# Attention of a streaming encoder layer: units of four key blocks, maxima between the scores, VectorE in written order

## The chip, the core and the metric

The kernel runs on one core of a Trainium2 chip. A core has TensorE (PE, matrix products into PSUM), VectorE (DVE), ScalarE (ACT) and GpSimd (POOL) for elementwise work, and SyncE (SP), whose queue issues the transfers between memory and SBUF. The metric is the device time of one execution in microseconds.

## The reference

One inference step of a layer with two branches, for a prompt of 2048 tokens and 64 decoded tokens that follow a cache of 512. One input projection (3080 columns) feeds an S5 branch (width 512) and an attention branch (8 heads of 64 with a forget bias); both are gated, concatenated, and go through one output projection. The part that the change touches:

```python
def _fox_attend(q, cum_q, pos_q, k, v, cum_k, pos_k):
    s = jnp.einsum('bqhd,bkhd->bhqk', q, k).astype(jnp.float32) * ATTN_SCALE
    s = s + jnp.transpose(cum_q, (0, 2, 1))[:, :, :, None] - jnp.transpose(cum_k, (0, 2, 1))[:, :, None, :]
    mask = pos_k[None, :] <= pos_q[:, None]
    s = jnp.where(mask[None, None], s, -jnp.inf)
    p = jax.nn.softmax(s, axis=-1)
    return jnp.einsum('bhqk,bkhd->bqhd', p.astype(v.dtype), v)
```

The prompt attends to itself, causally; the decoded tokens attend to the cache and to themselves. All is float32.

## The kernel before

The stages follow each other: input projection and the S5 scan (to about 724 us in the trace), the S5 branch's sigmoid gate, "GLU" (724 to 790), attention (790 to 1217), and the output product (to the end).

**Work of attention.** The heads are taken in four pairs `hp`, the two heads of a pair on two halves of the partitions or of PSUM. For each pair come five query tiles `qt`: 4 stands for the decoded tokens, 0 to 3 for 512 queries each of the prompt. Keys come in blocks of 128, four to a "kind" (the cache, a quarter of the prompt, or the new tokens). A tile's work per key block:

- *scores* (`scores`): four matmul pairs into a "twin", a PSUM tile [128, 2, 512] from a ring of three. Keys stand on the partitions. The pair `sm`, `kb` adds the biases and subtracts each query's maximum; `qs`, `ks` are the high and low parts of queries and keys (three products). A causal block gets mask products more. ScalarE takes the exponential of the twin into `p`. Scores are row-tiled (64x128: two matmuls on two halves of the rows).
- *values* (`mix`): the products of `p` with `vt`, column-tiled (128x64), gathered over the tile's blocks in one PSUM bank `po`. Two blocks form a unit (`PVG`), and the values of a unit come after the scores of the *next* one (`pend`).
- *additions*: the denominators need the sum of all `p`; VectorE and GpSimd add them in turn (`i % 2`, partial blocks on VectorE) into two `acc`, which are joined, and `sums` multiplies with ones, at a later unit. The result is scaled into `z` and stored for the output product.

**Maxima** (`maxima`): ahead of a tile's scores its maxima must be known. For 128 queries and a kind of keys, one matmul pair (high parts only) writes a twin, and VectorE adds the bias `cb` (loaded by SP and spread over the partitions) and takes the maximum, once for each head (line 1411, output `pb` into a scratch tile, `pm` the maximum). Two such steps go with each unit of two blocks (one after each block's scores), and two with each of the sixteen steps of GLU (`MXU`). When the last is done, `mq` is written, transposed on TensorE and copied to `sm`.

**Transposes** (`turn`): loaded keys and queries (`kn`) are transposed on TensorE into the PSUM bank `tr`; ScalarE copies the high part, VectorE subtracts for the low part (line 1375). One turn follows each unit, unless `sums` stands there.

**Order.** TensorE runs in the order in which the code is written (`Chain` with `strict`); on the other engines a scheduler orders the ready instructions. Buffers that are held for a time (`hold`, `claim`, `can`) are keyed by the tile's place in the order.

**Output weights.** Once nothing is left to load, the generator `Out.weights` is advanced by two steps after each unit: a weight tile is loaded into `ost` (a ring of three), split by a cast on ScalarE (`ohb`) and a subtraction on GpSimd (`olb`), two loads later. The output product itself begins after attention.

## Time and profile before

| | us |
|---|---|
| median of 3 runs (lowest, highest) | 1391.43 (1388.07, 1394.94) |
| profiled execution | 1393.23 |
| its span | 1391.4 |
| TensorE, VectorE, ScalarE, GpSimd busy | 1312.5, 968.5, 652.0, 520.5 |
| attention, 790 to 1217: TensorE, VectorE, ScalarE, GpSimd busy | 405.1, 317.0, 205.5, 163.9 |

The mean granted clock of TensorE is 0.981. Busy time on TensorE counts a matmul from its start to its modelled end, slow clock included. Line 154 is the chain's `matmul`, so groups of TensorE are told apart by their tiles: `twin<-sm,kb` begins a block of scores, `twin<-qs,ks` are its other products, `twin<-ks,qs` with 128 queries as weights is a maximum, `bank<-p,vt` are values, `bank<-ident,kn` and `bank<-identr,mq` transposes, `bank<-acc,ones` sums.

### The profile page before, as it was taken

What the parts mean: (1) busy time and instruction counts of PE and PEld (TensorE: products, weight loads), DVE (VectorE), ACT (ScalarE), POOL (GpSimd) and SP (SyncE); (2) the same over time, 40 slices, a digit from 0 to 9 for tenths busy, and PEclk for the clock granted to TensorE, in tenths of its full rate; (3) what the DMA queues carried; (4) which work ended last, traced back from release to release, by engine and by line L of the source; (5) the groups of instructions that cost most, each with busy time, mean ns of one, the idle gap of its engine ahead of it and who ended that gap; (6) DMA issues with size and microseconds to landing.
All of it is one profiled execution on the core that took longest, in us unless ns stands there. A gap on an engine that the chain in (4) does not pass through costs nothing.

```text
span 1391.4 us, 25886 instructions
## 1 busy us (share of the span) xinstructions
PE 1312.5 (94%) x9164; PEld 1031.9 (74%) x9164; DVE 968.5 (70%) x2404; ACT 652.0 (47%) x1710; POOL 520.5 (37%) x502
## 2 busy tenths in 40 slices
PE   5888999999999899999999899999999989898998
PEld 2886999998889899998879755555555554387887
DVE  3635896977877679864218877786787885446775
ACT  3645356567453576573315335445445445522211
POOL 1100254556534354452004113423423426743453
PEclk9899999999999999999999889999999999999999
DMA  9885333543546836446249624134121133495552
GB/s 342 318 309 124 100 86 94 154 123 107 163 133 217 282 110 180 145 141 196 84 138 291 202 73 121 32 91 125 43 70 48 40 65 79 146 330 169 182 164 78
DMA packets 249476, 204.92 MB, mean 147 GB/s; under 512 B 91296, under 2 KB 217340, under 8 KB 248322
## 3 DMA queue, kind: packets, MB, share of 16 engines
q1 hardware_dynamic: 249346, 203.27, 47.6%
q8 instruction: 72, 1.18, 0.4%
q14 instruction: 58, 0.48, 0.1%
HBM read 137.68 MB, written 65.53 MB: 146 GB/s over the span
## 4 chain that ended last, share of the span: by engine, by line
PE 63%; DVE 11%; DMA 6%; POOL 4%; issue 4%; ACT 3%; SPq 1%; DVEq 0%; ACTq 0%; POOLq 0%
PE low L154 25%; PE twin L154 13%; PE bank L154 12%; PE last L154 7%; PE glu L154 3%; DVE pb L1411 2%; PE bank L157 2%; DMA wst<-in_w_in_dram 1%; POOL qss L329 1%; POOL olb L205 1%; DMA lt<-t 1%; DVE acc L1489 1%; ACT p L354 1%; DVE ev L650 1%; DVE wlo L323 1%
## 5 line engine op out<-in xcount | busy, mean ns | idle before, releaser
L154 PE MATMUL low<-whi,h 128*128 128x256 f32 (+1 forms) x1584 | 296.3, 285 | 6.5 <-DVE th L609 3.5
L154 PE MATMUL low<-h,whi 128*128 128x256 f32 (+2 forms) x1152 | 277.6, 332 | 0.4 <-DVE h L323 0.3
L154 PEld LDWEIGHTS low<-whi,h 128*128 128x128 f32 x1584 | 247.9, 189 | 10.0 <-DVE th L609 3.7
L1411 DVE CUSTOM_DVE_ANT_0 pb<-twin,cb 128x512 bf16<-128x512 f32 (+3 forms) x328 | 199.9, 609 | 58.9 <-PE twin L154 49.1
L154 PE MATMUL low<-wlo,h 128*128 128x256 f32 (+1 forms) x816 | 229.1, 283 | 5.9 <-DVE wlo L323 5.9
L154 PEld LDWEIGHTS low<-h,whi 128*128 128x128 f32 x1152 | 195.5, 192 | 21.4 <-issue 2.8
L354 ACT ACTIVATE p<-twin 128x1024 f32<-128x1024 f32 (+3 forms) x180 | 149.7, 839 | 119.4 <-PE twin L154 107.2
L154 PE MATMUL low<-h,wlo 128*128 128x256 f32 (+2 forms) x576 | 188.2, 327 | 1.2 <-DVE wlo L323 1.2
L154 PEld LDWEIGHTS low<-wlo,h 128*128 128x128 f32 x816 | 154.3, 189 | 8.2 <-DVE wlo L323 7.7
L154 PE MATMUL bank<-p,vt 128*64 128x512 f32 (+3 forms) x704 | 142.5, 527 | 0.0
L154 PE MATMUL twin<-qs,ks 64*128 64x512 f32 (+3 forms) x1056 | 134.1, 359 | 0.0
L154 PEld LDWEIGHTS low<-h,wlo 128*128 128x128 f32 x576 | 110.3, 192 | 10.9 <-DVE wlo L323 2.6
L323 DVE TENSOR_TENSOR wlo<-wst,whi 128x512 fp32r<-128x512 f32 (+1 forms) x96 | 71.6, 752 | 59.9 <-ACT whi L319 59.7
L1489 DVE TENSOR_TENSOR acc<-acc,p 128x1024 f32<-128x1024 f32 (+4 forms) x88 | 90.2, 1025 | 30.5 <-ACT p L354 28.1
L329 POOL TENSOR_TENSOR qss<-qss,mhalf 128x4 f32<-128x4 f32 (+1 forms) x68 | 79.9, 1176 | 84.1 <-DVE qss L328 76.0
L154 PEld LDWEIGHTS twin<-qs,ks 64*128 64x128 f32 x1056 | 95.2, 191 | 11.0
L154 PE MATMUL twin<-sm,kb 64*128 64x512 f32 (+3 forms) x360 | 78.0, 428 | 21.2 <-DVE pm L1411 14.4
L319 ACT CAST whi<-wst 128x512 fp32r<-128x512 f32 (+1 forms) x96 | 58.7, 619 | 73.2 <-PE low L154 37.5
L154 PEld LDWEIGHTS bank<-p,vt 128*64 128x64 f32 x704 | 45.2, 140 | 63.8 <-issue 56.1
L205 POOL TENSOR_TENSOR x<-x,ot 128x512 f32<-128x512 f32 (+1 forms) x34 | 52.8, 1556 | 84.4 <-DVE ot L1816 79.7
L154 PEld LDWEIGHTS twin<-sm,kb 64*128 64x128 f32 x360 | 34.5, 187 | 61.8 <-DVE pm L1411 32.8
L646 ACT ACTIVATE hsq<-ev 128x64 bf16<-128x64 f32 (+1 forms) x272 | 69.7, 256 | 8.2
(437 smaller groups left out, 2634.2 us busy)
## 6 DMA issues: line engine op xcount, KB each, us to landing
wst<-in_w_in_dram SPq DMA_DIRECT2D x48, 512.0 KB
x<-in_x_prompt_dram SPq DMA_DIRECT2D x32, 512.0 KB
h<-h SPq DMA_DIRECT2D x16, 1024.0 KB
wada<-in_w_ada_dram SPq DMA_DIRECT2D x12, 1024.0 KB
cb<-cb_d SPq DMA_DIRECT2D x20, 512.0 KB
out_dram<-ev SPq DMA_DIRECT2D x64, 128.0 KB
out_dram<-x SPq DMA_DIRECT2D x32, 256.0 KB
z_d<-th SPq DMA_DIRECT2D x24, 256.0 KB
```

Source lines behind the costliest of these rows:

```text
L154: return self.keep(self.pe.matmul(*a, **kw))
L157: return self.keep(self.pe.transpose(*a, **kw))
L205: PL.tensor_tensor(out, x, y, op=op)
L319: i = S.copy(hi, x)
L323: V.tensor_tensor(lo, x, hi, op=ALU.subtract)
L329: PL.tensor_tensor(out, out, bc(mhalf[:out.shape[0]], list(out.shape)), op=ALU.pow)
L354: i = S.activation(out, x, func, **kw)
L646: S.activation(sq[:r], tv[:, h], AF.Square, accum_out=ss[:r, h:h + 1])
L650: V.tensor_tensor(tv, tv, e.bc(ss[:r].unsqueeze(2), [r, 4, HD]), op=ALU.mult)
L1411: V.tensor_tensor_reduce(b[:, :n], ps[:, h, :n], cb[:, h, :n], 1.0, NEG, ALU.add, ALU.max, accum_out=self.pm[:, t, h, pi:pi + 1])
L1489: (PL if j else V).tensor_tensor(y[:rows, :, c0:nq], x[:rows, :, c0:nq], p[:rows, :, :n], op=ALU.add)
```

## The change

A unit has four key blocks, and its values follow its own scores. A maximum may stand ahead of the first score, and after the second, third and fourth: `pace` issues it when a count (`need`, maxima still missing for the next tile over the units left) asks for it or when VectorE's reckoned backlog (`lag`) is below `LAG`. Then come up to two transposes into one twin (`turns`), then the unit's additions on VectorE and GpSimd, then the values, then the sums of an earlier tile. GpSimd gets five of eight additions, partial blocks too. The decoded tokens are no unit of their own any more: their scores, in two twins, and values stand inside the unit ahead of them in the order (`decoded`). VectorE runs in written order throughout attention; in the profile its lines there all become that of the chain. The bias `cb` is loaded for each kind of keys of each tile (44 loads of 512 KB instead of 20) into 4 buffers, where there were 6, and `p` has 8 buffers instead of 6. The output weights get 4 buffers `ost`, their casts come three loads later, a unit advances them by two steps and by four when all maxima are done, and then the subtraction is VectorE's. In GLU a second transpose may follow every other step.

```diff
-PVG = 2
+PVG = 4
+LAG = 4.6
...
 class Chain:
-    def matmul(self, *a, **kw):
-        return self.keep(self.pe.matmul(*a, **kw))
...
+    def __getattr__(self, name):
+        f = getattr(self.pe, name)
+        return lambda *a, **kw: self.keep(f(*a, **kw))
...
-    V, S, PL, PE = nc.vector, nc.scalar, nc.gpsimd, Chain(tc, nc.tensor, nosync)
+    S, PL = nc.scalar, nc.gpsimd
+    V, PE = Chain(tc, nc.vector, nosync), Chain(tc, nc.tensor, nosync)
...
-        for tag, kb, n in (("kw", 0.25, 4), ("vn", 0.5, 2), ("cw", 0.5, 2), ("cb", 4, 6), ("qs", 2, 12), ("sm", 2, 6),
+        for tag, kb, n in (("kw", 0.25, 4), ("vn", 0.5, 2), ("cw", 0.5, 2), ("cb", 4, 4), ("qs", 2, 12), ("sm", 2, 6),
...
-            self.order += [(hp, qt) for qt in (4, 0, 1, 2, 3)]
+            self.order += [(hp, qt) for qt in ((4, 0, 1, 2, 3) if hp else (0, 1, 4, 2, 3))]
...
+    def turns(self, apart=False):
+        n = self.due()
+        if n < 2 and not apart:
+            return self.turn()
+        ps = self.twin()
+        for evict in [self.turned(False, ps[:, h]) for h in range(min(n, 2))]:
+            evict()
...
+    def biases(self):
+        while len(self.bias_at) < len(self.jobs):
...
+            if not self.can("cw" if new else "cb", 1):
+                return
...
+            cb = self.bias_at[j] = self.claim([P, 2, w], "cw" if new else "cb", j, F32)
+            e.nc.sync.dma_start(cb, e.cb_d[2 * hp:2 * hp + 2, t0 * P:t0 * P + w].partition_broadcast(P))
...
+    def pace(self, most=1):
+        for _ in range(most):
+            if self.need <= 0 and self.lag >= LAG:
+                return
+            n = self.maxima()
+            if not n:
+                return
+            self.need -= 1
+            self.lag += 2 * n / 960 + 0.25 - n / 2400
...
+    def add(self, tile, i, p, rows, c0, n):
...
-        j = i % 2 if whole and not late else 0
+        j = int(i % 8 not in (0, 2, 5)) if not late and (whole or (acc[1] is not None and not tile.given[1])) else 0
...
+    def decoded(self, tile):
...
+            if kt > 1:
+                y = self.mem.tile([P, 2, 256], F32, tag="pd", name="pd")
+                e.V.tensor_tensor(y, p[:, :, :256], p[:, :, 256:], op=ALU.add)
...
     def run(self, out):
...
-        for tag, kb, n in (("p", 4, 6), ("acc", 4, 4), ("z", 2, 2), ("w", 2, 2)):
+        for tag, kb, n in (("p", 4, 8), ("acc", 4, 4), ("z", 2, 3), ("w", 2, 2), ("pn", 1, 1), ("pd", 2, 1)):
...
+        out.idle = lambda: self.job == len(self.jobs)
+        self.forced, self.delay, self.adds = 0, 1, []
+        e.V.strict = True
...
+            if qt == 4:
+                units[-1].append((i, blocks, True, True))
...
+            self.need = 0
+            for k in range(at + 1, len(units)):
+                n = self.left(units[k][-1][0])
+                if n > 0:
+                    self.need = -(-n // max(1, k - at - 1))
+                    break
+            groups = []
+            self.pace()
...
+                for j, (kd, t) in enumerate(blocks):
+                    groups[-1].append(self.scores(tiles[i], kd, t))
+                    if j:
+                        self.pace()
+            if self.need > 0:
+                self.pace()
+            self.turns(len(unit) > 1)
+            for x in self.adds:
+                self.add(*x)
+            self.adds = []
+            self.lag = max(0.0, self.lag + self.busy - 0.4 - sum(8.2 * x[4] for g in groups for x in g) / 2400)
+            for (i, blocks, first, last), group in reversed(list(zip(unit, groups))):
+                self.mix(tiles[i], group, first, last)
...
+            if not (self.todo or self.loaded):
+                self.give(out)
+                for _ in range(4 if self.job == len(self.jobs) else 2):
                     next(weights, None)
-                    next(weights, None)
...
-        mem.ring("ost", 2048, 3)
+        mem.ring("ost", 2048, 4)
...
-            e.split(st, h, l, keep=True)
+            e.split(st, h, l, el=e.V if self.idle() else None, keep=True)
...
-                if len(late) == 2:
+                if len(late) == 3:
                     part()
```

In the built programs attention has 90 groups of values before and 39 after. The maxima that GLU takes grow from 8616 to 9536 columns. Of the additions of whole blocks into `acc` VectorE has 38 before and 24 after, GpSimd 22 and 36; of partial ones (384, 256, 128 columns per head, and the decoded tokens' 64 rows) VectorE has 16, 15, 15 and 4 before, and 13, 8, 5 and none after, GpSimd none before and 3, 7, 10 after; the 4 first additions of 128 columns (`acc<-p,p`) of VectorE are gone. VectorE gets 4 `pd` and 6 `olb` more, GpSimd 6 `olb` fewer (10). Of VectorE's additions with two operands in SBUF (`pd` among them) 52 stand ahead of the last maximum after, 84 before.

TensorE, in a tile of 512 queries, before: the end of one block's scores, a maximum, the next block's scores, a maximum, sums, the two blocks of values of the unit before, and the next unit's first scores.

```order
L154 MATMUL twin_8167<-qs_3_8295,ks_12_8949 128x512 x2
L154 MATMUL twin_9004<-ks_12_8949,qs_6_8513 128x512 x2
L154 MATMUL twin_8163<-sm_1_8178,kb_0_7729 128x512 x2
L154 MATMUL twin_8163<-qs_2_8294,ks_12_8949 128x512 x2
L154 MATMUL twin_8163<-qs_2_8294,ks_13_8950 128x512 x2
L154 MATMUL twin_8163<-qs_3_8295,ks_12_8949 128x512 x2
L154 MATMUL twin_8167<-ks_14_9123,qs_6_8513 128x512 x2
L154 MATMUL bank_77<-acc_3_9279,ones_0_91 64x512 x2
L154 MATMUL bank_81<-p_0_9019,vt_0_9005 64x512 x2
L154 MATMUL bank_81<-p_1_9033,vt_0_9005 64x512 x2
L154 MATMUL twin_9004<-sm_1_8178,kb_0_7729 128x512 x2
L154 MATMUL twin_9004<-qs_2_8294,ks_14_9123 128x512 x2
```

TensorE in a like place after: the end of the scores of the unit's last block, a maximum, two transposes in one twin, four blocks of values, the sums, and a maximum ahead of the next scores.

```order
L156 MATMUL twin_9065<-qs_2_8218,ks_13_8871 128x512 x2
L156 MATMUL twin_9065<-qs_3_8219,ks_12_8870 128x512 x2
L156 MATMUL twin_8179<-ks_14_9168,qs_6_8546 128x512 x2
L156 MATMUL twin_8183<-identr_0_87,mq_188704_0_7733 73x128 x4
L156 MATMUL twin_8183<-ident_0_82,kn_2_8212 128x128 x4
L156 MATMUL bank_81<-p_6_9209,vt_2_9244 64x512 x2
L156 MATMUL bank_81<-p_7_9223,vt_2_9244 64x512 x2
L156 MATMUL bank_81<-p_0_9087,vt_2_9244 64x512 x2
L156 MATMUL bank_81<-p_1_9101,vt_2_9244 64x512 x2
L156 MATMUL bank_77<-acc_3_9487,ones_0_91 64x512 x2
L156 MATMUL twin_9065<-ks_14_9168,qs_6_8546 128x512 x2
```

Four blocks of values stand together instead of two, and between the two blocks of transposes and the values no other work comes. The maximum after the sums takes the next twin of the ring.

VectorE in a tile of 512 queries, before; an `ISA` row with two outputs is one maximum, the row after it the read of its result.

```order
L1411 ISA pb_0_8412,pm_0_8409<-twin_8163,cb_6_9121 128x512
L1411 ISA pm_0_8409 128x1
L1489 TENSOR_TENSOR acc_3_9279<-acc_3_9279,p_1_9033 128x1024
L1411 ISA pb_0_8412,pm_0_8409<-twin_8163,cb_6_9121 128x512
L1411 ISA pm_0_8409 128x1
L1411 ISA pb_0_8412,pm_0_8409<-twin_9004,cb_7_9224 128x128
L1411 ISA pm_0_8409 128x1
L1411 ISA pb_0_8412,pm_0_8409<-twin_9004,cb_7_9224 128x128
L1411 ISA pm_0_8409 128x1
L1411 ISA pb_0_8412,pm_0_8409<-twin_8167,cb_0_8190 128x512
L1411 ISA pm_0_8409 128x1
```

VectorE after, where a unit ends:

```order
L156 ISA pb_0_8363,pm_1_8479<-twin_8183,cb_0_8220 128x512
L156 ISA pm_1_8479 128x1
L156 ISA pb_0_8363,pm_1_8479<-twin_8179,cb_1_8222 128x128
L156 ISA pm_1_8479 128x1
L156 ISA pb_0_8363,pm_1_8479<-twin_8179,cb_1_8222 128x128
L156 ISA pm_1_8479 128x1
L156 TENSOR_TENSOR ks_3_8215<-twin_8183,ks_2_8214 128x512
L156 TENSOR_TENSOR qs_11_8815<-twin_8183,qs_10_8814 128x512
L156 TENSOR_TENSOR acc_2_9227<-p_6_9209,p_0_9087 128x1024
L156 ISA pb_0_8363,pm_1_8479<-twin_9065,cb_1_8222 128x256
L156 ISA pm_1_8479 128x1
```

Before, an addition stands between the two maxima of one twin. After, the two subtractions for the paired transposes and then the unit's addition stand behind all maxima of the unit and ahead of those of the next.

ScalarE in the last tiles, before: casts of output weights (`ohb`) between the exponentials (`p`), all from three buffers.

```order
L319 CAST ohb_197760_0_12497<-ost_0_12469 128x512
L319 CAST ohb_9728_0_12503<-ost_1_12471 128x512
L354 ACTIVATE p_4_9099<-twin_9004 128x1024
L354 ACTIVATE p_5_9137<-twin_8163 128x2x384
L319 CAST ohb_13824_0_12541<-ost_2_12501 128x512
L319 CAST ohb_17920_0_12546<-ost_0_12469 128x512
L354 ACTIVATE p_0_9019<-twin_8167 128x2x256
L354 ACTIVATE p_1_9033<-twin_9004 128x2x128
L319 CAST ohb_22016_0_12583<-ost_1_12471 128x512
L319 CAST ohb_1536_0_12588<-ost_2_12501 128x512
```

ScalarE in the last tiles, after:

```order
L354 ACTIVATE p_4_9185<-twin_8179 128x1024
L354 ACTIVATE p_5_9195<-twin_8183 128x1024
L354 ACTIVATE p_6_9209<-twin_8179 128x1024
L354 ACTIVATE p_7_9223<-twin_9065 128x1024
L1390 COPY sm_1_8194<-bank_77 73x512
L319 CAST ohb_37632_0_12585<-ost_2_11948 128x512
L319 CAST ohb_4864_0_12590<-ost_3_11954 128x512
L319 CAST ohb_41728_0_12595<-ost_0_11862 128x512
L319 CAST ohb_8960_0_12600<-ost_1_11864 128x512
L354 ACTIVATE p_0_9087<-twin_9065 128x1024
L354 ACTIVATE p_1_9101<-twin_8179 128x2x384
```

The casts stand behind four exponentials instead of two. The subtractions that free the buffers stand on VectorE here, behind the unit's additions:

```order
L156 TENSOR_TENSOR acc_0_9148<-acc_0_9148,p_5_9195 128x1024
L156 TENSOR_TENSOR acc_0_9148<-acc_0_9148,p_6_9209 128x1024
L156 TENSOR_TENSOR acc_0_9148<-acc_0_9148,p_7_9223 128x1024
L156 TENSOR_TENSOR olb_2816_0_12586<-ost_2_11948,ohb_37632_0_12585 128x512
L156 TENSOR_TENSOR olb_39680_0_12591<-ost_3_11954,ohb_4864_0_12590 128x512
L156 TENSOR_TENSOR olb_6912_0_12596<-ost_0_11862,ohb_41728_0_12595 128x512
L156 TENSOR_TENSOR olb_11008_0_12601<-ost_1_11864,ohb_8960_0_12600 128x512
L156 TENSOR_TENSOR acc_0_9148<-acc_0_9148,acc_1_9225 128x1024
```

Before, all sixteen of these were GpSimd's.

More of the change, by code (lines that the diff above doesn't have):

```diff
@@ L1300, in load @@
             new = kind == "n"
-            if not (self.can("kw" if new else "ks", 2) and self.can("cw" if new else "cb", 1)):
+            if not self.can("kw" if new else "ks", 2):
                 return
@@ L1519, in sums, with give @@
         e.nc.sync.dma_start(e.ma_d[P * tile.hp:P * tile.hp + P, :, 64 * tile.qt:64 * tile.qt + n // TC], tile.z)
+    def give(self, out):
+        if not self.given:
+            self.given.append(None)
+            out.mem.add(self.ring("kn"))
+            out.mem.add([(a / 1024, b / 1024) for a, b in self.mem.segs if b > a])
+            self.mem.segs = []
+        out.mem.add(self.spare("ks", "qs"))
+        if len(self.bias_at) == len(self.jobs):
+            out.mem.add(self.spare("cb"))
+        if self.job == len(self.jobs) and not self.smq:
+            out.mem.add(self.spare("sm"))
     def run(self, out):
@@ L1580, in run @@
+        if len(done) > 1:
+            self.sums(done.pop(0))
         out.mem.add(self.spare("vt"))
-        self.cur = self.seen = len(self.order)
-        out.mem.add(self.spare("cb", "ks", "qs", "sm"))
+        self.cur = len(self.order)
+        self.give(out)
         out.mem.join()
```

261 lines of the change are left out of this document (163 added, 98 removed).

## The prediction

> **What bounds the kernel now.** I read the busy times first, then the table by stretches, then the waits of TensorE, and last the order of time at the places where those waits lie. The columns of the table are stretch and length, busy time and count of each engine, granted clock, DMA share and GB/s.
>
> ```profile
> PE 1312.5 (94%) x9164; PEld 1031.9 (74%) x9164; DVE 968.5 (70%) x2404; ACT 652.0 (47%) x1710; POOL 520.5 (37%) x502
> ...
> 790.00:820.00 30.00, 25.02 (x192) 16.34 (x192) 20.16 (x63) 8.62 (x17) 1.79 (x3) 0.72 0.56 152
> 820.00:904.00 84.00, 83.91 (x659) 45.67 (x657) 66.52 (x178) 41.79 (x53) 32.66 (x15) 1.00 0.26 73
> 904.00:922.00 18.00, 16.20 (x166) 10.19 (x166) 16.82 (x48) 7.87 (x15) 4.10 (x5) 1.00 0.32 76
> 1165.00:1197.00 32.00, 27.06 (x182) 13.47 (x180) 15.66 (x11) 17.64 (x27) 25.68 (x15) 0.95 0.51 133
> 1197.00:1217.00 20.00, 17.38 (x120) 7.95 (x118) 11.07 (x11) 10.33 (x17) 13.52 (x7) 0.91 0.49 158
> 1217.00:1391.00 174.00, 166.33 (x718) 136.17 (x716) 111.67 (x139) 35.59 (x62) 73.46 (x49) 0.97 0.54 185
> 790.00:1217.00 427.00, 405.10 (x3213) 224.50 (x3213) 316.99 (x799) 205.54 (x288) 163.93 (x87) 0.97 0.31 83
> ```
>
> Attention runs from 790 to 1217, and the diff touches little else. TensorE is busy 405.1 of its 427 us. In the middle of a head pair (820 to 904) it has no hole, so only its own work can shrink there. At the start, at a change of the head pair (904 to 922, where VectorE is busy 16.8 of 18) and at the end it has holes, and the granted clock is 0.72 at the start and 0.91 at the end. The waits say whom it waits for (engine, line, releaser: us in total, times, longest), and the last two rows are ScalarE's and the DMA queue's in the same stretch:
>
> ```profile
> PE twin L154 <- DVE pm L1411: 14.4, 15, 3.2
> PE twin L154 <- ACT p L354: 6.4, 3, 2.6
> PE bank L154 <- DVE acc L1489: 1.1, 1, 1.1
> ACT ohb L319 <- DMA ost<-in_w_out_dram: 18.7, 8, 4.7
> SPq L1519 <- POOL z L205: 122.1, 17, 23.3
> ```
>
> Of the 22 us, 14.4 are waits for a maximum (a twin that VectorE has not read yet), and 6.4, in three waits, for an exponential. So the change can gain in four ways: fewer switches of TensorE between row and column tiling, the holes at the head changes, the end, and the start.
>
> **1. Fewer value groups.** A warm unit of two blocks in order of time (start, duration, instruction): scores, maximum, scores, maximum, values, transposes.
>
> ```profile
> 991.16 0.50 PE L154 MATMUL twin<-sm,kb 64*128 64x512 f32 x2
> 991.49 0.86 PE L154 MATMUL twin<-qs,ks 64*128 64x512 f32 x6
> 992.19 0.39 PE L154 MATMUL twin<-ks,qs 64*128 64x512 f32 x2
> 992.41 0.40 PE L154 MATMUL twin<-sm,kb 64*128 64x512 f32 x2
> 992.65 0.86 PE L154 MATMUL twin<-qs,ks 64*128 64x512 f32 x6
> 993.53 0.49 PE L154 MATMUL twin<-ks,qs 64*128 64x512 f32 x2
> 993.96 1.94 PE L154 MATMUL bank<-p,vt 128*64 128x512 f32 x8
> 995.83 0.48 PE L157 MATMUL bank<-identr,mq 128*73 128x128 f32 x4
> ```
>
> From start to start a maximum's pair takes 0.22 us among scores (992.19 to 992.41) and 0.43 ahead of values (993.53 to 993.96): 0.21 to get into the values. The first pair of scores takes 0.33 after the transposes (991.16 to 991.49) and 0.24 otherwise: 0.09 to get out. The values take 1.87; eight passes at the 0.22 of a 512-column pass are 1.76, so 0.1 more is the way out again. Together 0.39 per group. By the order of the built programs attention has 90 value groups before and 39 after, with the same multiplications: 51 x 0.39 = **-20 us**. Since the transposes stood at the same switch, pairing them adds nothing.
>
> **2. The head changes.** The 14.4 us less the 3.2 at 792 and the 2.5 of two more in the first 25 us leave 8.7 between 904 and 1146. There all maxima that the next head's first tiles need were still queued at one spot. Afterwards `pace` spreads them by need over the units before, and the decoded tokens have no unit with its own short scores. VectorE has room for that: 66.5 of 84 us between the head changes. I take all of it (the least would be nothing, if the waits only move into the units): **-9 us**.
>
> **3. The end.** A cast of an output weight that waits for its DMA stands ahead of the exponential in ScalarE's order:
>
> ```profile
> 1182.95 0.62 ACT L319 CAST ohb<-ost 128x512 fp32r<-128x512 f32 x1 [3.83 <-DMA ost<-in_w_out_dram]
> 1184.54 0.79 PE L154 MATMUL twin<-sm,kb 64*128 64x512 f32 x2 [2.65 <-ACT p L354]
> 1186.55 2.46 PE L154 MATMUL bank<-p,vt 128*64 128x512 f32 x8
> ```
>
> After the stall the eight values take 2.46 instead of 1.94, the granted clock being 0.95. The loads come late because a buffer of `ost` is free only after GpSimd's subtraction `olb`. With four buffers, casts that begin a unit after their load, and six of the sixteen subtractions moved to VectorE (busy 15.7 of 32 us there), I take the 6.4 us of waits and about 3 of slowed clock (0.05 x 32 + 0.09 x 20 = 3.4): **-9.4 us**.
>
> **4. The start.** After the wait of 3.2 us the same work runs slower for some ten us:
>
> ```profile
> 792.30 0.48 PE L154 MATMUL twin<-sm,kb 64*128 64x128 f32 x2 [3.22 <-DVE pm L1411]
> 792.57 0.84 PE L154 MATMUL twin<-qs,ks 64*128 64x128 f32 x6
> 798.67 1.12 PE L154 MATMUL bank<-p,vt 128*64 128x128 f32 x8
> ...
> 908.93 0.60 PE L154 MATMUL bank<-p,vt 128*64 128x128 f32 x8
> ```
>
> The values of four short blocks take 1.12 us at 798 and 0.60 at 908, and the scores of a short block 0.84 against 0.50 for their six. Some 12 us between 792 and 805 are thus 6 too many, and with 5.7 of waits the start costs 12. The decoded tokens no longer come first, and the GLU stage does a few more maxima (9536 columns instead of 8616 by the order); but VectorE still has the first tile's maxima on its hands. I take half of it, between nothing and 12: **-6 us**. The Trainium skill (TensorE: Matmul & The Clock Gate, Part 1) says that an idle window of about 3.4 us halves the clock and that a busy one restores it; the 1.12 against 0.60 agrees with half, and by that rule a wait cut below the window would give the whole 6 of slow clock back, so that the sum would be 3 lower.
>
> **5. New waits.** With a unit that runs M S S M S M S M (M a maximum, S a block's scores) on a ring of three twins a maximum's twin must be read before the third next piece can start, and VectorE, now in written order, has the unit's additions between the last maxima of one unit and the first of the next. Below stands no cost (820 to 904 shows none), above a whole addition each unit. The first row is a maximum's (687 ns), the next an addition's, the last GpSimd's; the columns are instruction, shape, count, busy us, mean ns and the idle time before:
>
> ```profile
> L1411 DVE CUSTOM_DVE_ANT_0 pb<-twin,cb 128x512 bf16<-128x512 f32 x211 | 145.0, 687 | 31.5 <-PE twin L154 25.5 <-DVE pm L1411 0.5 <-PE bank L154 0.3
> L1489 DVE TENSOR_TENSOR acc<-acc,p 128x1024 f32<-128x1024 f32 x38 | 50.4, 1327 | 25.5 <-ACT p L354 23.7
> ...
> L1489 DVE TENSOR_TENSOR acc<-acc,p 128x768 f32<-128x768 f32 x16 | 16.1, 1008 | 0.2
> ...
> L1489 DVE TENSOR_TENSOR acc<-acc,p 128x512 f32<-128x512 f32 x15 | 11.2, 748 | 2.3 <-ACT p L354 2.2
> ...
> L1489 DVE TENSOR_TENSOR acc<-acc,p 128x256 f32<-128x256 f32 x15 | 7.2, 480 | 0.4 <-ACT p L354 0.2
> ...
> L1489 DVE TENSOR_TENSOR acc<-acc,p 64x256 f32<-64x256 f32 x4 | 5.2, 1310 | 2.1 <-ACT p L354 2.1
> ...
> L1489 POOL TENSOR_TENSOR acc<-acc,p 128x1024 f32<-128x1024 f32 x22 | 52.3, 2378 | 44.1 <-ACT p L354 44.1
> ```
>
> I take half a maximum, 0.35 us, in each of 39 units, being nearer to the dense stretch, which ran without holes: **+13.6 us** (0 to 39 x 1.33 = 52).
>
> **6. The rest at nothing.** VectorE loses 14 large additions (14 x 1.33 = 19 us) and 28 small ones (3 of 768 columns, 7 of 512, 14 of 256 and the four of 64 rows: 20 us by the rows); it gains four `pd` and six subtractions, all of 128x512 and so about 0.75 each. Before the last two tiles that leaves it 28 us less. GpSimd gains 14 large and 20 small ones; 2.5 of 2.38 us per unit is 6 of the unit's 9, so it holds. 24 more loads of `cb` of 512 KB each lie on queues that the table shows 0.31 busy; on SP they stand ahead of the loads of `vt` and `kn`, which have a unit of about 9 us for cover. SP already sits up to 23.3 us behind a store without TensorE showing any wait for a DMA.
>
> The sum: 20 + 9 + 9.4 + 6 less 13.6 is 30.8 off the profiled execution's 1393.2, so 1362.4. The median of the runs is 1.8 below that execution: 1360.6, said as **1360 us**.
>
> **Rivals.** *Additions blocked by GpSimd.* The four 64x256 additions take 1310 ns, a larger one of 128x256 480: those ran beside a GpSimd instruction, as here, where an addition of 1.33 us in the mean took 2.31 and ended after `z`:
>
> ```profile
> 1188.17 1.58 POOL L205 TENSOR_TENSOR z<-w,z 128x512 f32<-128x512 f32 x1
> 1188.53 2.31 DVE L1489 TENSOR_TENSOR acc<-acc,p 128x1024 f32<-128x1024 f32 x1 [2.54 <-ACT p L354]
> ```
>
> Now both engines' additions are issued together at the unit's end, and behind VectorE's stand the next maxima. Up to 1165 VectorE has 290 us of work (317.0 less 15.7 and 11.1), 262 after term 6; TensorE has 361, and 335 after terms 1 and 4. Of the 73 us of room I call half usable, since it doesn't all lie where the additions do. 52 of VectorE's additions stand there in the new order. From 1.6 us of wait each ((45 + 37) / 52) the gains are gone; the whole 2.38 each gives 124 - 37 = 87, so 1393.2 - 44.4 + 87 - 1.8 = 1434 us: slower. Against it: the maxima behind which the additions stand leave GpSimd time to finish first, and most of its additions wait for an exponential. The Trainium skill (SBUF — State Buffer, Who interferes with whom) has this as a rule: a VectorE instruction with two SBUF inputs and a GpSimd one that reads SBUF exclude each other for a whole instruction; the 2.31 agrees.
>
> *No new wait, start healed:* term 5 at zero and all 12 of the start: 1391.4 - 44.4 - 6 = 1341.
>
> *Loads late behind `cb`:* a load of `cb` waits on SP for VectorE's reading, now in written order, and holds up about 20 loads of `vt`. At over 45 / 20 = 2.3 us of TensorE's time each, slower; the lag that `pace` allows is 4.6, less than the cover, so hardly.
>
> *The gain is given back:* new waits of 0.95 to 1.3 us per unit (37 to 51 us), nearly the whole addition each time: 1391.4 - 44.4 + 37 to 51, 1384 to 1398, no change. For it speaks that at a head change, where VectorE is as full as a unit's end will be, single waits already reach that size; against it that `pace` puts a maximum's due time by VectorE's lag.
>
> **How the numbers follow.** What a measurement can tell from no change is about 0.5%, 7 us: 1384.5 to 1398.4. The forecast's case (1343 to 1384) has 0.66; the larger gain (below 1343) 0.14; given back, 0.11; slower by blocked additions or late loads 0.09. So faster 0.80, same 0.11, slower 0.09. The range leaves out the top of the given-back case and what is slower, and a little below 1335: 1335 to 1387.
>
> **What would show it.** Right: 39 value groups with their maxima at 0.22 in between; no wait for `ost` before an exponential after 1130; no wait of TensorE over 1 us at the three head changes; VectorE's additions at 1.2 to 1.3 us. Wrong: additions of 2 us and more beside GpSimd, TensorE's waits for `pm` above 30 us in all, a wait for `vt`, or a first unit that still stalls over 3 us with slow pieces after it.

## The result, and the profile after

The change made the kernel slower: 1403.93 us, median of 9 runs (1400.48 to 1412.29), against 1393.40 of 9 runs of before (1388.00 to 1395.75). The ratio is 1.0089, 95% interval 1.0063 to 1.0115. The forecast was 1360, with 1335 to 1387. The profiled execution took 1406.79 us, span 1404.9. Among the experiments below, e4 and e11 have one run each above 2500 us; without it their medians are 1393.26 and 1386.96.

The table by stretches (columns as before): GLU and what follows it up to the first score; attention's first 30 us; attention while there are maxima; its end; the output product; and attention as a whole.

```profile
728.00:804.00 76.00, 66.48 (x549) 59.24 (x551) 63.81 (x160) 31.88 (x63) 18.01 (x12) 1.00 0.81 247
804.00:834.00 30.00, 26.66 (x234) 16.51 (x230) 19.70 (x50) 11.65 (x16) 8.30 (x5) 0.89 0.28 81
834.00:1187.00 353.00, 327.19 (x2683) 191.75 (x2681) 250.79 (x645) 163.19 (x224) 176.89 (x96) 0.96 0.38 106
1187.00:1229.00 42.00, 40.56 (x308) 21.74 (x304) 30.01 (x34) 21.18 (x29) 16.23 (x7) 1.00 0.37 85
1229.00:1405.00 176.00, 166.12 (x716) 136.27 (x716) 116.47 (x141) 37.27 (x66) 74.29 (x49) 0.98 0.56 189
804.00:1229.00 425.00, 394.40 (x3219) 230.01 (x3215) 300.51 (x727) 196.02 (x268) 201.43 (x107) 0.96 0.37 102
```

From the first GLU matmul to the first score it was 67.3 us before (724.96 to 792.30) and is 75.5 now (728.32 to 803.84); attention was 424.8 and is 424.9; the output product 174.3 and 176.2. The GLU stage itself begins 3.4 later, a drift that arises in the stages ahead of it, where the diff touches nothing; in the kernels below that stage begins at 722.3 to 726.2. So attention, where 31 us were to be gained, gained nothing, and the stage ahead of it lost 8.

The busy share of attention fell all the same (394.4 of 425 against 405.1 of 427). What took its place is seen in the clock, 0.96 in the long middle stretch where it had been 1.00, and in the waits (engine, line, releaser: total, times, longest):

```profile
PE twin L156 <- DVE pm L156: 28.9, 48, 3.6
PE twin L156 <- ACT p L354: 3.1, 6, 0.9
PE bank L156 <- ACT p L354: 1.2, 3, 0.4
```

TensorE waited 15 times for a maximum before, 14.4 us; now 48 times, 28.9. Each number holds the one wait just ahead of the first score (3.2 and 3.6 us), which lies at the end of the GLU stage; attention's own waits for maxima are 11.2 and 25.3 us, the longest now 1.95. To keep the parts apart I cut attention, from the first score to the last product with ones (the sums), into stretches of 2 us and summed three things: the idle time, the busy time times what the granted clock lacks to 1 ("lost to the clock"), and the rest, work at full clock. The same sum stands here for the experiments that follow, each from its own profile.

| us | attention | idle | lost to the clock | work at full clock |
|---|---|---|---|---|
| before | 424.8 | 19.6 | 11.4 | 393.8 |
| after | 424.9 | 30.4 | 16.1 | 378.4 |
| e1, fewer additions on GpSimd | 413.6 | 28.6 | 6.6 | 378.5 |
| e3, VectorE scheduled | 480.2 | 65.6 | 37.4 | 377.2 |
| e4, 18 maxima in GLU | 422.4 | 29.7 | 9.7 | 382.9 |
| e7, units of two | 450.8 | 49.2 | 16.1 | 385.4 |
| e8, before with the new tail | 413.6 | 12.5 | 8.1 | 393.0 |
| e9, e1 and e4 | 415.0 | 27.9 | 3.2 | 383.9 |
| e10, half maxima | 395.7 | 14.5 | 3.3 | 377.9 |

The work fell by 15.4 us as it should. Idle time (+10.8) and clock (+4.7, though start and end had got better) took all of it back.

How that goes is seen best at a head change. In order of time, VectorE's and GpSimd's additions at the end of a full unit, and VectorE's next maximum:

```profile
896.97 2.36 POOL L1574 TENSOR_TENSOR acc<-acc,p 128x1024 f32<-128x1024 f32 x1 [0.51 <-ACT p L354]
897.71 3.96 DVE L156 TENSOR_TENSOR acc<-acc,p 128x1024 f32<-128x1024 f32 x2
901.58 0.68 DVE L156 CUSTOM_DVE_ANT_0 pb<-twin,cb 128x512 bf16<-128x512 f32 x1
```

TensorE in the unit that follows, the last of the head pair, with its short diagonal blocks:

```profile
899.51 0.50 PE L156 MATMUL twin<-ks,qs 64*128 64x512 f32 x2
...
903.06 0.50 PE L156 MATMUL twin<-ks,qs 64*128 64x512 f32 x2 [1.13 <-DVE pm L156]
...
905.10 0.33 PE L156 MATMUL twin<-sm,kb 64*128 64x128 f32 x2 [0.64 <-DVE pm L156]
905.26 0.50 PE L156 MATMUL twin<-qs,ks 64*128 64x128 f32 x6
...
906.70 0.33 PE L156 MATMUL twin<-sm,kb 64*128 64x128 f32 x2 [0.57 <-DVE pm L156]
906.86 0.68 PE L156 MATMUL twin<-qs,ks 64*128 64x128 f32 x6
...
907.55 0.85 PE L156 MATMUL twin<-qs,ks 64*128 64x128 f32 x6
...
911.27 1.97 PE L156 MATMUL bank<-p,vt 128*64 128x128 f32 x16 [0.39 <-ACT p L354]
```

Two additions of 1.22 us each take 3.96: they begin 0.74 us after GpSimd's, and from the end of that one (899.33) to theirs (901.67) are 2.34 us, nearly the time of two. The maximum whose matmuls ran at 899.51 is read only from 901.58, three waits for maxima follow, and from 907 the six products of a short block take 0.85 us instead of 0.50: the clock has halved, for some ten us. The blocks from 906.70 on are those of the decoded tokens, which the change put into this unit, so that it holds all the short scores of a head change. In the long middle stretch the granted clock is at half from 907 to 917, 1020 to 1026 and 1129 to 1139, once at each of the three head changes; it is so twice more in attention's first 30 us, at 805 to 808 and 818 to 822.

### The profile page after: what moved, and what is told of

Same layout as the page of the kernel before. It is cut to its first block, busy times and chain, and to the rows that moved or that the text cites. A ratio compares the mean times of both kernels' runs of the same rounds, so it can differ in the third digit from the quotient of the medians.

```text
span 1404.9 us, 25978 instructions
## 1 busy us (share of the span) xinstructions
PE 1307.1 (93%) x9196; PEld 1040.9 (74%) x9196; DVE 968.8 (69%) x2380; ACT 645.6 (46%) x1698; POOL 559.8 (40%) x526
## 5 line engine op out<-in xcount | busy, mean ns | idle before, releaser
L354 ACT ACTIVATE p<-twin 128x1024 f32<-128x1024 f32 (+3 forms) x164 | 143.1, 900 | 107.2 <-PE twin L156 98.8
L156 PE MATMUL bank<-p,vt 128*64 128x512 f32 (+3 forms) x704 | 137.0, 535 | 1.2 <-ACT p L354 1.2
L1574 POOL TENSOR_TENSOR acc<-acc,p 128x1024 f32<-128x1024 f32 (+3 forms) x56 | 110.9, 1980 | 32.6 <-ACT p L354 30.2
L156 PEld LDWEIGHTS twin<-qs,ks 64*128 64x128 f32 x1056 | 96.3, 195 | 12.5
L156 PEld LDWEIGHTS bank<-p,vt 128*64 128x64 f32 x704 | 49.2, 146 | 72.2 <-issue 63.0
L156 PE MATMUL twin<-ks,qs 64*128 64x512 f32 (+3 forms) x328 | 71.2, 435 | 21.5 <-DVE pm L156 21.2
L156 PE MATMUL twin<-sm,kb 64*128 64x512 f32 (+3 forms) x360 | 74.2, 408 | 13.4 <-DVE pm L156 9.9
```

The lines of the kernel that those rows point to most:

```text
L156: return lambda *a, **kw: self.keep(f(*a, **kw))
L354: i = S.activation(out, x, func, **kw)
L1574: (PL if j else V).tensor_tensor(y[:rows, :, c0:nq], x[:rows, :, c0:nq], p[:rows, :, :n], op=ALU.add)
```

## Experiments

Two theories at first: the exclusion of VectorE's and GpSimd's additions, and the order itself (three twins, written order). A third was that the GLU stage pays for its six more maxima.

**e1: most of GpSimd's additions left out.**

```diff
+        if j and i < tile.nb - 4 and not tile.end:
+            if acc[1] is None:
+                acc[1] = self.mem.tile([P, 2, 512], F32, tag="acc", name="acc")
+                PL.memset(acc[1], 0.0)
+            return
```

> The changed kernel with 34 of GpSimd's 48 additions of whole blocks left out (those of blocks before the diagonal block in all but the last two tiles; 10 clears of 128x1024 stand in their place, and the denominators are then too small). VectorE's instructions and their order stay as they are. Exclusion theory (VectorE's additions at the end of a unit wait until GpSimd's end, the maxima behind them come late, TensorE stalls at the head changes and its clock drops): VectorE's 26 large additions before 1187 us fall from 49.3 us to about 35, TensorE's waits for maxima from 28.9 to about 12, the granted clock between 834 and 1187 rises from 0.96 to 0.99, and the time falls by 15 to 28 us, to 1376 to 1389. Order theory (the ring of three twins and the written order make the waits, whatever GpSimd does): waits stay above 24 us and the time within 6 us of 1404.

1391.77 us, ratio to before 1.0008 (0.9988 to 1.0028): 12 us less than the change. VectorE's large additions up to the last maximum, in the changed kernel and (the last two rows) here, with count, busy us, mean ns:

```profile
L156 DVE TENSOR_TENSOR acc<-acc,p 128x1024 f32<-128x1024 f32 x15 | 29.4, 1960 | 0.1
L156 DVE TENSOR_TENSOR acc<-p,p 128x1024 f32<-128x1024 f32 x11 | 19.9, 1809 | 0.0
```

```profile
L156 DVE TENSOR_TENSOR acc<-acc,p 128x1024 f32<-128x1024 f32 x15 | 18.3, 1219 | 0.1
L156 DVE TENSOR_TENSOR acc<-p,p 128x1024 f32<-128x1024 f32 x11 | 13.4, 1218 | 0.0
```

The exclusion is shown: 49.3 us become 31.7 when most of GpSimd's additions are gone, 17.6 us of VectorE's time. But attention's own waits for maxima fall only from 25.3 to 21.4. What fell is the loss to the clock, from 16.1 to 6.6 us. TensorE's waits at the three head changes became smaller (2.7 to 1.3 us, 2.3 to 1.5, 2.3 to 1.6) and at the last two the clock held; at the first, with the least waiting, it was still at half for 7 us. The mean clock of the ten runs is 0.981 to 0.988, that of the change's nine 0.971 to 0.982, so the clock is better in more than this one profile. So each theory had half: GpSimd's additions cost the 12 us, most of it by way of the clock, and most of the waits have another cause. That the longer additions are the only link between the two was not tried.

**e2: an addition after each block.**

```diff
                     if j:
+                        self.add(*self.adds.pop(0))
                         self.pace()
```

> The changed kernel with each block's addition issued after the next block's scores, ahead of the next maximum, instead of all at the end of the unit. Exclusion theory: VectorE's addition then mostly falls before GpSimd's of the next block, so the 49.3 us of large additions fall below 40, the waits for maxima below 20 us, and the time to 1380 to 1395. Order theory: an addition ahead of a maximum delays that maximum's twin by 1.2 us in the middle of the unit, the waits grow, 1405 to 1420.

1431.28 us, 1.0278 (1.0248 to 1.0308). The time is above both expectations, and the order theory has the direction: an addition ahead of a maximum holds up that maximum's twin. TensorE waited 38.9 us for maxima in attention. Of the large additions the eleven of the form `acc<-p,p` took 1.22 us each instead of 1.81, the other seventeen 1.9 us, much as in the change, and VectorE waited 6.6 us for exponentials ahead of them.

**e3: VectorE's order left to the scheduler.**

```diff
-        e.V.strict = True
```

> The changed kernel with VectorE's order left to the scheduler as in the kernel before, all else the same. Order theory: the waits for maxima fall from 28.9 us to below 15 and the time to 1375 to 1390. Exclusion theory: the scheduler knows nothing of GpSimd's hold, so additions still run long (over 42 us for the 26 large ones) and the time stays at 1395 to 1410.

1462.78 us, 1.0504 (1.0483 to 1.0525), which neither theory had: waits for maxima of 60.9 us (57.3 without the one at the start). The written order isn't the fault of the change; it saves 59 us in it. The scheduler puts additions ahead of maxima, as e2 does: up to the last maximum 51 of VectorE's 56 additions stand directly between two reads of maxima here, 5 of 52 in the change. Whether that makes all of the 59 us wasn't tried.

**e4: 18 maxima in GLU, as before, instead of 24.**

```diff
             for _ in range(MXU):
-                self.maxima()
+                if self.given2 < 18 and self.maxima():
+                    self.given2 += 1
```

> The changed kernel with 18 maxima steps within the sixteen steps of the GLU stage, as many as before, instead of 24. Theory that these six make the stage longer: the stage goes from 70.4 us to about 63 (62.6 before); the six fall into attention, where each costs TensorE 0.3 and VectorE 1.5 us: the first units stall up to 5 us longer, and the total is 1397 to 1402. Rival (the stage is longer because VectorE's order or the transposes changed): it stays above 68 and the time at 1404 or more.

1394.70 us, 1.0014 (0.9994 to 1.0034), 9 us less. The waits in that stage, changed kernel and before, and VectorE's long maxima there (count, busy us, mean ns), say why:

```profile
PE twin L156 <- DVE pm L156: 9.1, 7, 3.6
```

```profile
PE twin L154 <- DVE pm L1411: 4.3, 3, 3.2
```

```profile
L156 DVE CUSTOM_DVE_ANT_0 pb<-twin,cb 128x512 bf16<-128x512 f32 x32 | 21.9, 684 | 1.2 <-PE twin L156 0.4
```

```profile
L1411 DVE CUSTOM_DVE_ANT_0 pb<-twin,cb 128x512 bf16<-128x512 f32 x22 | 15.1, 685 | 1.9 <-PE twin L154 1.5
```

Six steps more (each reads once for each head) are ten reads of 512 columns and two of 384, in a stage in which VectorE also has the gate's own products and only two twins stand between it and TensorE. Before, VectorE was already busy 55.5 of 67 us there:

```profile
725.00:792.00 67.00, 62.09 (x519) 56.78 (x519) 55.51 (x129) 30.84 (x60) 19.20 (x14) 1.00 0.81 246
```

With 18, the GLU matmuls take 66.1 us instead of 70.4 and the first score follows 0.9 us after them instead of 5.1, with no slow clock:

```profile
789.00:819.00 30.00, 26.80 (x276) 16.96 (x274) 24.07 (x63) 14.26 (x20) 8.33 (x5) 1.00 0.42 117
```

(GLU's end is counted here at the start of its last matmul.) The six maxima put back into attention made it no longer (422.4 us).

**e5: GpSimd takes the first two blocks of a unit, VectorE the last two** (with 18 maxima in GLU).

```diff
-        j = int(i % 8 not in (0, 2, 5)) if not late ...
+        j = int(i == 1 or i > 3 and i % 4 < 2) if not late ...
```

> The kernel with 18 maxima in GLU (1394.7 us), with GpSimd's additions moved to the first two blocks of a unit and VectorE's to the last two, so that GpSimd has mostly finished when VectorE's start; VectorE has two whole additions per unit instead of one and a half. Exclusion theory: VectorE's whole additions fall from 1.86 us each to 1.3 or less, the waits of TensorE for maxima from 22.0 to below 16 us, time 1380 to 1390. Rival (VectorE's load counts, not the exclusion): the extra additions (some 10 x 1.2 us) make it 1395 to 1405.

1420.24 us, 1.0206 (1.0182 to 1.0230). The additions got shorter as the exclusion theory has it (43 large ones, 57.7 us, 1.34 each instead of 1.86), and it was 25 us slower all the same: VectorE had fifteen more of them and more of the partial ones, 86 us of additions in all instead of 69, and the waits for maxima went from 22.0 to 29.1. But the run does not show that VectorE's load makes the 25 us. `lag` counts VectorE's additions, so the edit also makes `pace` issue maxima later: in the traces 66 maxima of attention stand ahead of the nineteenth group of values here, and 70 in the kernel with 18. TensorE waits 8.4 us for `mq` in two waits, as in e13, where only the planner's bound was lowered (65 maxima at that place, 8.0 us) and the time was 1415.36.

**e6: no maximum between the third and the fourth scores** (with 18 in GLU); what the count asks for stands at the unit's end.

```diff
-                    if j:
+                    if j % 2:
                         self.pace()
-            if self.need > 0:
-                self.pace()
+            for _ in range(3):
+                if self.need > 0:
+                    self.pace()
```

> The kernel with 18 maxima in GLU (1394.7 us), with no maximum between a unit's third and fourth scores; those that the count still asks for stand together at the unit's end (up to four). Ring theory (with M S M S two maxima and one block of scores share three twins, so that the scores must wait for a maximum, 8.6 us in all): that group of waits falls below 3 us, the maxima at the end are covered by the values (3.7 us), and the time falls to 1385 to 1391. Rival (the count of maxima and VectorE's speed set the waits, wherever they stand): the waits move to the transposes and to the next unit's maxima and the time stays at 1392 to 1402.

1412.18 us, 1.0153 (1.0121 to 1.0185). Sorted by the three pieces ahead of it, TensorE's idle time before scores behind M S M went from 8.6 us to nothing, as the ring theory says; but that before a maximum behind M S S went from 7.7 to 25.3. The waits moved, the rival holds.

**e7: units of two blocks in the changed kernel.**

```diff
-PVG = 4
+PVG = 2
```

> The changed kernel with units of two blocks (PVG 2), all else as changed. Theory that the larger unit saves TensorE's switches but makes new waits: the busy work of TensorE in attention grows by about 16 us at full clock, while its waits for maxima fall from 28.9 to below 12 us and the clock stays at 0.98 or more in the middle: time within 8 us of 1404. Rival (the larger unit is pure gain): 1416 or more.

1432.16 us, 1.0292 (1.0269 to 1.0315). The larger unit is worth 28 us inside the changed kernel, whose other parts were written for it. Only 7 of these are work (385.4 against 378.4), not 16; the rest is idle time, as with M S S M (M a maximum, S a block's scores) the values stand close behind the last scores and wait for exponentials (7.2 us in 16 waits) and for `vt` (6.3), and the waits for maxima don't fall (31.4 against 25.3).

**e8: the kernel before with the change's tail only** (four `ost`, three loads' delay, subtractions on VectorE).

```diff
-        yield from wait(5)
-        mem.ring("ost", 2048, 3)
+        yield from wait(6)
+        mem.ring("ost", 2048, 4)
...
-                if len(late) == 2:
+                if len(late) == 3:
...
-            e.split(st, h, l, keep=True)
+            e.split(st, h, l, el=e.V if self.idle() else None, keep=True)
```

> The kernel before with only the change's treatment of the output weights: four buffers ost, casts three loads later, the subtractions on VectorE once no maximum, load or transpose is left. Theory: the 6.4 us of TensorE's waits for exponentials behind casts in the last 40 us of attention go and its clock stays full, so the time falls by 5 to 9 us, to 1383 to 1387. Rival: the loads are late for another reason (SP's order, memory), less than 2 us.

1381.52 us, 0.9931 (0.9911 to 0.9951): the only part of the change that was tried by itself, and a kernel that beats both. The end of attention, from the last maximum on, here and in the kernel before:

```profile
1154.00:1206.00 52.00, 51.58 (x368) 25.80 (x366) 40.75 (x42) 33.67 (x47) 18.46 (x8) 1.00 0.46 138
```

```profile
1153.00:1217.00 64.00, 56.44 (x378) 27.20 (x374) 32.20 (x31) 35.68 (x51) 45.69 (x24) 0.95 0.44 122
```

Eleven us shorter (the two windows do not begin at quite the same place), TensorE nearly without holes and at full clock; GpSimd has 27 us less to do there, VectorE 8.5 more. The output product then starts 4 us later after the last value than before, which takes 2 back.

**e9: e1 and e4 together.**

> Both together: 34 of GpSimd's additions left out as in e1, and 18 maxima in GLU as in e4. If the two losses are separate (12 us of exclusion, 9 us of GLU), the time is 1380 to 1386. If they are one (the six maxima only move the same shortage of VectorE), 1389 or more.

1387.17 us, 0.9969 (0.9951 to 0.9987), between the two expectations: of 12 and 9 us together 17 are gained. They are separate for the most part.

**e10: maxima at half their columns on VectorE.**

```diff
+            r = slice(n // 2 if kind != qt and kind != "n" and qt < 4 else 0, n)
-            V.tensor_tensor_reduce(b[:, :n], ps[:, h, :n], cb[:, h, :n], 1.0, NEG, ALU.add, ALU.max,
+            V.tensor_tensor_reduce(b[:, r], ps[:, h, r], cb[:, h, r], 1.0, NEG, ALU.add, ALU.max,
```

> The changed kernel in which a maximum over keys other than the diagonal quarter and the decoded tokens' reads half the columns on VectorE (0.42 instead of 0.69 us each, the matmuls as before; the bound on the scores is then taken from half of those keys). Theory that VectorE's speed within a unit makes what is left (four blocks of scores and four maxima take TensorE 4.6 us, VectorE 5.9 us for the maxima alone, with only three twins between them): waits for maxima fall from 28.9 to below 10 us, the clock in the middle to 0.99 or more, and the time to 1365 to 1380. Rival (additions and the exclusion alone make the waits): above 1392.

1371.95 us, 0.9842 (0.9821 to 0.9862), 32 us less than the change with the same matmuls in the same order. The waits, and attention while there are maxima:

```profile
PE twin L156 <- DVE pm L156: 8.2, 18, 1.6
PE twin L156 <- ACT p L354: 3.4, 6, 0.9
```

```profile
831.00:1154.00 323.00, 310.43 (x2635) 182.11 (x2631) 211.82 (x640) 160.50 (x220) 178.05 (x96) 0.99 0.40 114
```

Here GpSimd's additions are all there and VectorE's large ones are as long as in the changed kernel (51.5 us), and most of attention's waits for maxima are gone nevertheless, 8.2 us instead of 25.3. So they hang on the time that VectorE takes for the maxima. Two things stay open. The kernel before was not run with half maxima; it too waits for maxima, so not all of the 32 us need be a loss of the change. And the GLU stage got no shorter (76.0 us from its first matmul to the first score, though VectorE is busy 58 us in it instead of 64): the wait of 3.6 us ahead of the first score is still there, and the clock is 0.95.

VectorE's busy share in the changed kernel is 71% of the middle stretch (250.8 of 353), so it isn't full. That it is full in the wrong part of a unit is an argument from rows, and was not tried apart. A unit that ran here without a wait gives TensorE's side, from its first maximum to its last one:

```profile
1035.69 0.50 PE L156 MATMUL twin<-ks,qs 64*128 64x512 f32 x2
...
1040.55 0.75 PE L156 MATMUL twin<-ks,qs 64*128 64x512 f32 x4
```

The last row is two maxima, of which the first is the unit's fourth. With it, four blocks of scores and four maxima take TensorE 5.2 us. VectorE, with whole maxima, needs 0.73 us from one head's to the next:

```profile
893.08 0.69 DVE L156 CUSTOM_DVE_ANT_0 pb<-twin,cb 128x512 bf16<-128x512 f32 x1 [0.67 <-PE twin L156]
893.69 0.08 DVE L156 DVE_READ_ACCUMULATOR2_ANT pm<- 128x1 f32 x1
893.81 0.69 DVE L156 CUSTOM_DVE_ANT_0 pb<-twin,cb 128x512 bf16<-128x512 f32 x1
```

That makes 5.9 us for the four maxima, and with three twins it can fall behind by no more than a maximum or two before TensorE stops. The values, 3.6 us in which VectorE could catch up, come after all four. With units of two, values of 1.87 us stood behind every two maxima.

**e11: GpSimd takes six of eight additions** (with 18 in GLU; some denominators of the prompt change with it).

```diff
-        j = int(i % 8 not in (0, 2, 5)) if not late ...
+        j = int(i % 8 not in (0, 4)) if not late ...
```

> The kernel with 18 maxima in GLU (1394.7 us), with GpSimd taking six of eight additions instead of five. VectorE has about a dozen additions fewer (1.2 to 1.9 us each), GpSimd some 7 us of additions in a unit of 9. Theory of exclusion by count: the waits for maxima fall by 4 to 8 us, 1385 to 1391. Rival: GpSimd is now nearly always adding, so each remaining addition of VectorE waits about 1.2 us longer, and the values or the exponentials wait for p: 1393 or more.

1388.26 us, 0.9969 (0.9948 to 0.9989): waits for maxima 18.5 us instead of 22.0, 6 us gained, as the theory has it. VectorE's large additions up to the last maximum are 22 and 33.2 us instead of 28 and 52.2; TensorE's order of maxima is that of the kernel with 18, so here the planner plays no part.

**e12: e8 without the two maxima in the last step of GLU.**

> The kernel before with the change's tail (1381.5 us) and without the two maxima in the last step of GLU. Theory that the 3.2 us stall at the start comes from these two (VectorE is then behind by the gate's own work) and that the half clock after it comes from the stall: the stall falls below 1 us and the clock between 792 and 822 from 0.72 to above 0.9: 1371 to 1377. Rival: the stall moves to the first tiles, whose maxima are then late: 1379 to 1385.

1382.11 us, 0.9923 (0.9897 to 0.9950), no different from e8. The first score follows the last GLU matmul after 0.7 us instead of 4.8, but attention takes 420.4 us instead of 413.6: the waits come in the first tiles, and the clock is at half there and after a head change. The rival holds.

**e13 and e14: the planner's allowed backlog, 2.5 and 7.0 instead of 4.6** (with 18 in GLU).

> The kernel with 18 maxima in GLU (1394.7 us) with LAG 2.5 instead of 4.6: a maximum that the count does not ask for is issued only when VectorE's reckoned backlog is small. If VectorE is overfilled in the middle of a head pair: waits fall from 22.0 to below 17 us, 1385 to 1391. If the head changes are short of early maxima: waits rise above 25 us and the time to 1398 to 1408.

> The kernel with 18 maxima in GLU (1394.7 us) with LAG 7.0: more maxima early. If the head changes are short of early maxima: waits below 18 us, 1386 to 1391. If VectorE is overfilled: waits above 25 us, 1398 to 1408. If the planner only moves the same waits (VectorE's work per unit is what counts): both runs stay within 4 us of 1394.7.

1415.36 us, 1.0177 (1.0157 to 1.0196), and 1393.00, 1.0014 (0.9997 to 1.0030). With less backlog the maxima are late: TensorE waits 8 us for `mq`, in two waits. With more, waits are the same (22.6). A higher bound for the planner gains nothing, so its 4.6 was no part of the loss.

## Why the prediction was wrong

The steps that failed are term 4, which put GLU's further maxima at nothing; terms 2 and 5, which took TensorE's waits for maxima in attention too small; and the clock, which the sum had only getting better. Term by term:

- **Term 1 (-20): nearly right.** Attention's work fell by 15.4 us at full clock. e7 puts only 7 of it on the size of the unit: its trace has 40 groups of values more, so a group costs under 0.2 us and not the 0.39 read from single rows. What of the rest is the paired transposes and the decoded tokens inside units was not tried apart.
- **Term 2 (-9 at the head changes): wrong.** "VectorE has room for that: 66.5 of 84 us" was read from a mean over a long stretch. The waits at the head changes stayed: 1.13, 0.64 and 0.57 us within 5 us at the first, with VectorE late out of the unit before and many short scores in this one. And the clock halves, which no term had: up to 14 us in the middle stretch (an estimate, 0.04 x 353).
- **Term 3 (-9.4 at the end): right.** e8 alone gives 10 us; ScalarE's waits for `ost` fall from 18.7 to 3.0 us, TensorE waits for no exponential there, and the clock is at 1.00.
- **Term 4 (-6 at the start): wrong in sign.** GLU's further maxima were put at nothing without a reason: I gave "a few more maxima" no price, and the count was wrong too. Up to the end of GLU the programs have 20 and 26 of these steps, 7616 and 10560 columns, not 8616 and 9536. VectorE was busy 55.5 us of 67 there already, and the first score still waited 3.6 us, with half clock after it, which the prediction had named as a sign of being wrong. It costs 9 us (e4).
- **Term 5 (+13.6 of new waits): mis-sized.** Terms 2 and 5 together have TensorE's waits for maxima grow by 4.6 us; attention's own grew by 14.1 (11.2 to 25.3). I took half a maximum per unit from a dense stretch without holes; there, values followed every second maximum. Comparing the two engines between two groups of values, 5.2 us of TensorE's with 5.9 of VectorE's, would have told that VectorE falls behind inside a unit, ahead of any addition: 0.7 us in each of 39 units at most, 27 us, less what the ring absorbs (an estimate).
- **Term 6 (additions at nothing) and the first rival.** The rival's mechanism came true, below its own threshold: 26 large additions take 0.68 us longer each in the mean, less than the 1.6 from which the gains would be gone, and GpSimd's additions cost 12 us (e1). I had written that the maxima ahead of them leave GpSimd time to finish; the addition at 897.71, 0.74 us after GpSimd's start, is the counterexample. The page SBUF — State Buffer of the Trainium skill (Who interferes with whom) was the rule that spoke against the change, and e1 agrees with it: without GpSimd's additions VectorE's take 1.22 us. The prediction's own row fits less well: that addition ended 0.73 us after `z`, sooner than a whole one of 1.22 us could. I gave the rival a small chance, and it was the ordinary case.
- The rival *the gain is given back* is nearest to what happened, though 1404 lies above its 1384 to 1398: 10.8 us more of idle time and 4.7 of slow clock ate term 1, and GLU took more. A clock made worse was in none of my cases; I had it only as something the change would heal.

In sum, the forecast was 30.8 us less and the two profiled executions differ by 13.5 more, 44.3 apart. Attention's work at full clock fell by 15.4 instead of 20, which is 4.6 short. Its idle time grew by 10.8 where terms 2 to 5 had about 5 less, 15.6 short, and the loss to the clock grew by 4.7 where terms 3 and 4 had 6 less, 10.7 short. The GLU stage took 8.2 us more, for which no term stood. Another 5.3 lie where no term speaks: 3.4 ahead of GLU and 1.9 in the output product. What the experiments take away (12 us in e1, 9 in e4, 32 in e10) overlaps and can't be added up to this.

## What to carry to other kernels

Grouping work to save switches also groups the cover of another engine: compare the two engines' times between two covers, with the depth of the ring that lies between them, not their busy shares over a stage. Two engines whose additions contend lengthen them when they are handed them at the same moment (17.6 us here), though the one way of parting them that was tried without leaving any out (e5) did not pay. Work that is moved out of a stall should be priced in the stage that it goes to. Of a change with several parts, the parts may be of both signs; here the tail alone gains 10 us (e8).

## What the runs showed of the hardware

TensorE's clock halved after waits none of which exceeded 1.2 us (2.3 us of idle time within 5 us at 902 to 907), and stayed at half for some ten us, while similar gaps in the kernel before (1.06 and 1.39 within 13 us at 1009 to 1022) left it at 1.00. In e1 waits of 0.31 and 0.57 us were followed by half clock at the first head change (from 902), and waits of 0.30 and 0.53, and of 0.30 and 0.60, at the other two were not: the size of the waits alone does not tell where the clock falls. The mean clock of the 9 runs of the changed kernel goes from 0.971 (1412.29 us) to 0.982 (1400.48), so the loss also varies from run to run. The Trainium skill (TensorE: Matmul & The Clock Gate, Part 1) speaks of an idle window of about 3.4 us; no wait at these places is that long. What exactly makes the clock fall was not tried.
